# Two layers of a hybrid diffusion trunk on one core: when the neighbourhood biases are asked for

## The chip, the cores and the metric

One core of a Trainium2 chip runs the whole program: TensorE (PE, with its weight loads as PEld), VectorE (DVE), ScalarE (ACT), GpSimd (POOL), SyncE (SP) and 16 DMA engines that all queues share. The metric is device time in microseconds (us) of one execution; lower is better. Of the runs shown the median counts.

## The reference, cut to what matters

Two layers over 256 latent tokens and, in the first layer alone, 256 context tokens, width 1024. Each layer multiplies the modulated, normalised tokens by one input projection and splits the result into three groups of heads: windowed attention (4 heads, here two pairs, A(0) and A(1)), a state space scan (8 heads, gated by `z`), and neighbourhood attention (4 heads, two pairs, N(0) and N(1)). For a neighbourhood head

```
sc = einsum(q, k) * scale + bias[rpb]     # 256 x 256, -1e30 outside the window
p  = softmax(concat([sc, s_ctx]))         # s_ctx: scores against 256 context tokens
o  = p_loc @ v + p_ctx @ v_ctx
```

The bias depends on weights alone, so its 256 x 256 table per head is laid out ahead of time and lies in device memory as `in_nab_dram`. The three groups are concatenated and multiplied by an output projection; then follow a router and a mixture of 32 gated experts (per token two of the eight experts of one group). The six shift, scale and gate rows of each layer (`mods` in the code) are the product of the conditioning with an 1024 x 6144 matrix, streamed from memory in slabs of 1 MB.

## The kernel before, in words

`mixers(l)` (l is 0 for the first layer, 1 for the second) does a layer's heads, `projection_and_experts(l)` what follows. Everything is unrolled; a planner (the framework's scheduler) simulates the program with costs of its own, and writes a fixed order for each engine: an instruction that is earlier in the program has priority among those whose inputs are ready in that simulation. On the chip each engine, and each queue of transfers, keeps that order and waits at whatever is not there yet.

One pair of heads is `attn_pair` (L797 to L845). For each of two blocks of 128 queries: scores of both heads by TensorE into two PSUM banks `sc`, for N pairs the bias added by VectorE (L815, one 128 x 512 instruction per block), the maximum (L817), `exp` by ScalarE into `pr` (L827), the division (L835), four transposes by TensorE into PSUM bank `tp` (L838), and a copy of these into a buffer `PT` (L839, by a helper that lets ScalarE, L238, and VectorE, L240, take turns). After both blocks 16 matmuls multiply `PT` with the values (L843, into `tp` again), and a copy takes the result to `oT`. `tp` is one bank, and the transposes of the output gate (`natural(9, z_post)`, L753) and of the state space norm (`ssd_gate`, L778 and L783) use it as well.

`PT` buffers have the tag `t4`, of which there are four (L273). A pair takes two. The biases `nb` (one tile of 128 x 2 x 2 x 256 for a pair, 0.5 MB) take one each, and so do the masks `M` of the state space scan, four for each of its chunks, which are done before attention begins. A tile gets its buffer in the order in which the program asks for tiles of that tag, and waits until one is free.

`attn_N(i)` (L860) asks for its bias at its own start: a tile `nb`, and two transfers of 256 KB on ScalarE's queue (L863). In the second layer the order of the program is A(0), three steps of `mods`, A(1), three steps of `mods`, N(0), three steps, `natural(9, z_post)`, `ssd_gate(0)`, N(1), and the rest of `mods`. A step of `mods` is eight matmuls (L116, L119) on one slab `m`; there is one buffer for `m`, so the next slab is loaded (L1662, on SP's queue) only when these are done. SP's queue also carries the weights: of the output projection (L88) and of the experts (L1004).

The output projection of the second layer starts inside this stretch: its first products (L1197) need A's and N(0)'s outputs, the following ones (L1206 to L1208) the gated state space output.

Of the kernel before, what the change touches and what calls it, by code (L numbers as in the profile page):

```python
# [44 lines left out]
def backbone(ctx: ExitStack, tc, I, out, dbg=None):  # L45
    nc = tc.nc
# [213 lines left out]
    def mixers(l):  # L260
# [3 lines left out]
        with ExitStack() as es:  # L264
# [7 lines left out]
            def t4(shape, name, dtype=F32):  # L272
                return tp.tile([P] + shape, dtype, tag="t4", name=name, bufs=4)  # L273
# [466 lines left out]
            def z_tile(i, p):  # L740
                silu_half(oT(2 + i), p, NTK)

            def natural(u, post):

                ws = [wunit(l, u), wunit(l, u + 1)]
                outs = [ps("mm"), ps("mm")]
                wN(ws, 512, outs)
                for t, p in enumerate(outs):
                    y = s2([512], "yn")
                    dst = post(y, p)  # L750
                    tr = ps("tp", (P, 4, P))
                    for c in range(4):
                        T.transpose(tr[:, c, :], y[:, c * P:(c + 1) * P], ident)  # L753
                    for j, d_ in enumerate(dst):
                        n = 4 // len(dst)
                        pcopy(d_[:, :, t * P:(t + 1) * P], tr[:, j * n:(j + 1) * n, :])
# [9 lines left out]
            def ssd_gate(s):  # L766
                seg = slice(s * 256, (s + 1) * 256)
                pn = ps("tp")
                y2s = []
                for g in range(2):  # L770
                    zs = oT(2 + 2 * g, seg, 2)
                    V.tensor_tensor(zs, zs, xc[:, 2 * g:2 * g + 2, seg], op=ALU.mult)
                    y2 = s2([2, 256], "y2")
                    S.activation(y2, zs, AF.Square)
                    y2s.append(y2)
                for i in range(2):
                    for ct in range(4):
                        T.matmul(pn[:, i:i + 1], y2s[ct // 2][:, ct % 2, i * P:(i + 1) * P], ones[:, 0:1],  # L778
                                 start=(ct == 0), stop=(ct == 3))
                rn = rstd_of(sm, pn[:, 0:2], 512, 2)  # L780
                pb = ps("tp")
                for i in range(2):
                    T.matmul(pb[:, i * P:(i + 1) * P], rn[:, i:i + 1].to_broadcast([P, P]), ident,  # L783
                             start=True, stop=True)
                for ct in range(4):
                    V.scalar_tensor_tensor(oT(2 + ct, seg), oT(2 + ct, seg), gcol[:, ct:ct + 1], pb[:, 0:256],
                                           op0=ALU.mult, op1=ALU.mult)


            def rope(x_):  # L790
                sh = s2([256], "sh")
                V.stream_shuffle(sh, x_, [i ^ 16 for i in range(32)])
                V.tensor_tensor(sh, sh, M_("sin"), op=ALU.mult)
                V.tensor_tensor(x_, x_, M_("cos"), op=ALU.mult)
                V.tensor_tensor(x_, x_, sh, op=ALU.add)
# [59 lines left out]
            def attn_A(i):  # L855
                attn_pair(kA, 0, (0, 64), i, sinks=snk[:, i:i + 3:2], wmask=True)
                if need_ctx:
                    attn_pair(kA, 1, (0, 64), i, sinks=snk[:, i:i + 3:2])

            def attn_N(i):  # L860
                nb = t4([2, 2, 256], "nb")
                for hf in range(2):
                    nc.scalar.dma_start(nb[:, hf], I["nab"][l, 2 * i + hf])  # L863
                vo = (128 + 128 * i, 128 + 128 * i + 64)
                attn_pair(kN[:, i], 0, vo, 6 + i, bias=nb)
                if need_ctx:
                    attn_pair(kN[:, i], 1, vo, 6 + i)

            def q_tile(i, p):
                S.activation(oT(i), p, AF.Copy, scale=0.125)  # L870

            if need_ctx:
                tl = Tiles([(5, 0), (5, 1), (6, 0), (6, 1), (7, 0), (7, 1), (8, 0), (8, 1), (9, 0), (9, 1), (10, 0)])

                def tile_():
                    p = tl.next()
                    mods(l, 1)
                    return p

                S.copy(kA, tile_())  # L880
                rope(kA[:, 0:256])
                q_tile(0, tile_())
                rope(oT(0, slice(0, 256)))
                q_tile(1, tile_())
                rope(oT(1, slice(0, 256)))
                S.copy(kN[:, 0], tile_())
                attn_A(0)
                attn_A(1)
                q_tile(6, tile_())
                q_tile(7, tile_())  # L890
                S.copy(kN[:, 1], tile_())
                attn_N(0)
                for i in range(4):
                    z_tile(i, tile_())
                ssd_gate(0)
                ssd_gate(1)
                attn_N(1)
            else:
                tl = Tiles([(5, 0), (5, 1), (6, 0)])
                S.copy(kA, tl.next())  # L900
                rope(kA[:, 0:256])
                S.copy(kN[:, 0], tl.next())
                S.copy(kN[:, 1], tl.next())
                mods(l, 2)
                natural(7, q_post)
                mods(l, 2)
                rope(oT(0, slice(0, 256)))
                rope(oT(1, slice(0, 256)))
                attn_A(0)
                mods(l, 3)  # L910
                attn_A(1)
                mods(l, 3)
                attn_N(0)
                mods(l, 3)
                natural(9, z_post)
                ssd_gate(0)
                attn_N(1)
# [752 lines left out]
    def mods(l, n):  # L1670
        for _ in range(n):
            next(rest[l], None)

    for l in range(2):
        oT = mixers(l)
        projection_and_experts(l, oT)
# [163 lines left out]
```

## Time and profile before

| what | value |
|---|---|
| median of 3 runs | 1119.57 us (1114.42 to 1122.86) |
| the profiled execution | 1124.72 us, of which span 1122.8 us |
| mean granted TensorE clock | 0.953 of full |
| PE busy | 1005.9 us, 90% of the span |
| DVE, ACT, POOL busy | 589.0, 280.5, 187.3 us |
| moved by DMA | 321.69 MB, mean 286 GB/s |

The profiled execution is 5.15 us longer than the median, so a sum made in its trace is a difference, to be taken from either. The granted clock is in tenths or hundredths of full speed: 1.00 is 2.4 GHz, 0.50 is 1.2 GHz. In the bracket behind a row stands how long its engine was idle just before it and what ended that.

### The profile page before, as it was taken

The page shows a single profiled execution, that of the slowest core. Times are in us where ns is not written, and L with a number is a line of the kernel's source. Part 1 is how long each engine was busy: PE and PEld are TensorE (multiplying, and loading weights), DVE is VectorE, ACT ScalarE, POOL GpSimd, SP SyncE. Part 2 cuts the span into 40 slices and gives each one's busy share as a digit, 9 for nine tenths or more (in the row PEclk, how much of TensorE's full clock was granted, in tenths as well). Part 3 has the DMA queues.
Part 4 walks back from the last instruction along what each step waited for, and adds up shares of the span by engine and source line. Part 5 has one row for each costly group of instructions (what it writes and reads, how often), then busy time and mean ns, then how long its engine had stood idle before and what let it go on. Part 6 is the DMA issues. An engine that isn't in the chain of part 4 may idle for free. (4 is left out here: it accounts for less than half of the span.)

```text
span 1122.8 us, 13571 instructions
## 1 busy us (share of the span) xinstructions
PE 1005.9 (90%) x5041; PEld 533.5 (48%) x5041; DVE 589.0 (52%) x1208; ACT 280.5 (25%) x567; POOL 187.3 (17%) x181
## 2 busy tenths in 40 slices
PE   6996899999998699988898798999789799999995
PEld 4684455456565233322343586564355444444342
DVE  5679695763557334322366687766434522322353
ACT  3242111442421112111122552133321211111112
POOL 2106270000214211111121404300010100000011
PEclk9997999999999799999999899899888899999998
DMA  9756545438195899999998534346748689999992
GB/s 378 287 214 244 225 151 185 154 136 330 65 382 207 295 405 424 424 425 425 426 415 313 182 113 150 130 149 220 306 153 360 239 344 424 424 425 424 424 400 81
DMA packets 60009, 321.69 MB, mean 286 GB/s; under 512 B 11899, under 2 KB 12795, under 8 KB 26584
## 3 DMA queue, kind: packets, MB, share of 16 engines
q1 hardware_dynamic: 51152, 305.57, 68.7%
q0 software_dynamic: 6048, 11.08, 2.7%
q10 hardware_dynamic: 2728, 4.02, 1.0%
q8 instruction: 44, 0.72, 0.3%
q14 instruction: 37, 0.30, 0.1%
HBM read 316.84 MB, written 22.09 MB: 302 GB/s over the span
## 5 line engine op out<-in xcount | busy, mean ns | idle before, releaser
L389 PE MATMUL mm<-x,sp 128*128 128x512 f32 (+1 forms) x176 | 73.5, 418 | 0.1
L391 PE MATMUL mm<-x,sp 128*128 128x512 f32 (+1 forms) x176 | 72.3, 413 | 0.3 <-DVE sp L249 0.3
L390 PE MATMUL mm<-x,sp 128*128 128x512 f32 (+1 forms) x176 | 71.5, 407 | 0.6 <-DVE alg L547 0.4
L1407 PE MATMUL mm<-w,xT 128*64 128x512 f32 x208 | 62.7, 596 | 6.1 <-DMA w<-in_wexp_dram 6.1
L1407 PE MATMUL mm<-w,xg__7943 128*64 128x512 f32 x216 | 66.0, 596 | 0.0
L1474 POOL DMA_INDIRECT yd<-y,irow x24 | 23.8, 991 | 215.6 <-DVE y L1473 206.6
L1414 DVE SCALAR_TENSOR_TENSOR hg<-hg,mm 128x256 f32<-128x256 f32 x32 | 13.4, 418 | 77.3 <-ACT hg L1413 77.3
L248 ACT CAST sp<-w 128x1024 fp32r<-128x1024 f32 (+1 forms) x42 | 42.5, 1013 | 34.7 <-PE mm L391 11.5
L249 DVE TENSOR_TENSOR sp<-w,sp 128x1024 fp32r<-128x1024 f32 (+1 forms) x36 | 44.8, 1246 | 9.6 <-ACT sp L248 9.5
L1413 ACT ACTIVATE hg<-mm 128x256 f32<-128x256 f32 x32 | 12.3, 384 | 147.9 <-PE mm L1407 147.9
L116 PE MATMUL mod<-m,cc 128*32 128x512 f32 x80 | 42.7, 616 | 5.3 <-DMA m<-in_wmod_dram 3.2
L240 DVE COPY xT<-sp 128x512 f32<-128x512 f32 x16 | 11.0, 690 | 67.3 <-PE sp L1399 67.3
L1407 PE MATMUL mm<-x,xg__7943 128*64 128x512 f32 x128 | 44.7, 597 | 0.0
L119 PE MATMUL mod<-m,cc 128*32 128x512 f32 x240 | 43.2, 616 | 0.0
L218 POOL TENSOR_TENSOR rs<-ms,nhalf 128x1 f32<-128x1 f32 (+2 forms) x13 | 9.3, 713 | 196.4 <-DVE mx L822 111.0
L389 PEld LDWEIGHTS mm<-x,sp 128*128 128x128 f32 x176 | 34.1, 194 | 15.4 <-issue 8.0
L827 ACT ACTIVATE pr<-sc,mx 128x512 f32<-128x512 f32 (+1 forms) x48 | 29.3, 616 | 46.8 <-DVE mx L822 43.8
L391 PEld LDWEIGHTS mm<-x,sp 128*128 128x128 f32 x176 | 34.1, 194 | 11.9 <-issue 5.6
L566 DVE SCALAR_TENSOR_TENSOR yh<-xp,cw,yh 128x512 f32<-128x512 f32 (+1 forms) x48 | 35.0, 728 | 8.8 <-ACT yh L564 7.2
L390 PEld LDWEIGHTS mm<-x,sp 128*128 128x128 f32 x176 | 34.2, 195 | 9.6 <-issue 4.0
L1322 POOL DMA_INDIRECT xg__2845<-h2d,itok x16 | 16.9, 1055 | 112.5 <-PE sp L1399 101.3
L1407 PEld LDWEIGHTS mm<-w,xg__7943 128*64 128x64 f32 x216 | 19.3, 137 | 31.5 <-issue 30.2
(1054 smaller groups left out, 2443.4 us busy)
## 6 DMA issues: line engine op xcount, KB each, us to landing
w<-in_wexp_dram SPq DMA_DIRECT2D x74, 1024.0 KB
x<-in_wexp_dram SPq DMA_DIRECT2D x46, 1024.0 KB
m<-in_wmod_dram SPq DMA_DIRECT2D x42, 1024.0 KB
w<-in_win_dram SPq DMA_DIRECT2D x21, 1024.0 KB
sp<-in_wexp_dram SPq DMA_DIRECT2D x20, 1024.0 KB
tb<-in_wexp_dram SPq DMA_DIRECT2D x11, 1024.0 KB
m<-in_wexp_dram SPq DMA_DIRECT2D x10, 1024.0 KB
xn<-in_wexp_dram SPq DMA_DIRECT2D x8, 1024.0 KB
```

Of the source, the lines that this page charges most:

```text
L116: line(first())
L119: line(other())
L248: S.copy(wh, w)
L249: eng.tensor_tensor(wl, w, wh.bitcast(F32), op=ALU.subtract)
L389: T.matmul(p[:, :n], wh[:, k], xh(k, slice(0, n))[:, 0], start=(k == 0), stop=False)
L390: T.matmul(p[:, :n], wh[:, k], xl(k, slice(0, n))[:, 0], start=False, stop=False)
L391: T.matmul(p[:, :n], wl[:, k], xh(k, slice(0, n))[:, 0], start=False, stop=(k == KD - 1))
L566: V.scalar_tensor_tensor(yh[:, :ns], xp[:, :ns, k:k + 256], cw[:, ct, k:k + 1], yh[:, :ns], op0=ALU.mult, op1=ALU.add)
L827: S.activation(pr[:, :n], sc[:, hf, :n], AF.Exp, bias=mx[:, hf:hf + 1], accum_out=l_[:, hf:hf + 1])
L1322: fetch_line(G.indirect_dma_start(xg_[:, p_ % 2, :], None, h2d[0:nt * P, :], bass.IndirectOffsetOnAxis(ap=itok[:, p_:p_ + 1], axis=0), bou ...
L1407: behind(T.matmul(ph[64 * e:64 * e + 64, :], xT[:, k, 64 * e:64 * e + 64], ws[e][k // 4][k % 4 // 2][:, k % 2 * 512:k % 2 * 512 + 512], st ...
L1474: fetch_line(G.indirect_dma_start(yd[l][0:2 * nt * P, :], bass.IndirectOffsetOnAxis(ap=irow[:, p_:p_ + 1], axis=0), y, None, bounds_check= ...
```

## The change

A function `bias_N` asks for the biases of the pairs that it is given, and `attn_N` takes the tile from a table. In the second layer both are asked for behind A(0) and ahead of A(1), so that they lie in two of the four `t4` buffers while A(1) and N(0) run; in the first layer that of N(0) is asked for between A(0) and A(1), and that of N(1) right behind N(0). What is computed is the same.

```diff
+            nbs = {}
+
+            def bias_N(*which):
+
+                for i in which:
+                    nbs[i] = t4([2, 2, 256], "nb")
+                    for hf in range(2):
+                        nc.scalar.dma_start(nbs[i][:, hf], I["nab"][l, 2 * i + hf])
+
             def attn_N(i):
-                nb = t4([2, 2, 256], "nb")
-                for hf in range(2):
-                    nc.scalar.dma_start(nb[:, hf], I["nab"][l, 2 * i + hf])
+                nb = nbs[i]
...
                 attn_A(0)
+                bias_N(0)
                 attn_A(1)
                 q_tile(6, tile_())
                 q_tile(7, tile_())
                 S.copy(kN[:, 1], tile_())
                 attn_N(0)
+                bias_N(1)
...
                 attn_A(0)
                 mods(l, 3)
+                bias_N(0, 1)
                 attn_A(1)
```

## Rows read from the trace of the kernel before

**Rows 1.** Tile view of the bias, whole execution: cause, us idle, times.

```profile
DMA nb<-in_nab_dram: 10.6, 2
```

**Rows 2.** Chain of waits, second layer: start us, us, what.

```profile
795.90 10.27 DMA nb<-in_nab_dram
```

**Rows 3.** Timeline of DVE, second layer: start us, us, instruction, [idle before].

```profile
770.50 0.68 DVE L240 COPY PT<-tp 128x512 f32<-128x512 f32 x1
...
780.42 0.68 DVE L240 COPY PT<-tp 128x512 f32<-128x512 f32 x1
...
786.91 1.30 DVE L815 TENSOR_TENSOR sc<-sc,nb 128x512 f32<-128x512 f32 x2 [1.66 <-DMA nb<-in_nab_dram]
...
789.25 0.41 DVE L240 COPY oA<-tp 128x256 f32<-128x256 f32 x1
...
806.25 1.30 DVE L815 TENSOR_TENSOR sc<-sc,nb 128x512 f32<-128x512 f32 x2 [8.94 <-DMA nb<-in_nab_dram]
```

**Rows 4.** Timeline of PE (matmuls), second layer, same columns.

```profile
776.27 1.95 PE L843 MATMUL tp<-PT,vt 128*64 128x256 f32 x16
778.58 0.62 PE L116 MATMUL mod<-m,cc 128*32 128x512 f32 x1
792.20 0.62 PE L116 MATMUL mod<-m,cc 128*32 128x512 f32 x1 [0.78 <-DMA m<-in_wmod_dram]
...
799.25 0.66 PE L838 MATMUL tp<-cst,pr 128*128 128x128 f32 x4
799.74 1.88 PE L1197 MATMUL mm<-w,oA 128*128 128x512 f32 x4
808.19 3.68 PE L843 MATMUL tp<-PT,vt 128*64 128x256 f32 x16 [6.57 <-DVE PT L240]
811.80 2.74 PE L1197 MATMUL mm<-w,oA 128*128 128x512 f32 x4
...
816.63 0.62 PE L116 MATMUL mod<-m,cc 128*32 128x512 f32 x1
...
820.35 3.58 PE L778 MATMUL tp<-masks,y 128*128 128x1 f32 x16 [2.06 <-ACT y L774]
```

**Rows 5.** Stretches: PE, PEld, DVE, ACT, POOL busy us, clock, DMA share, GB/s.

```profile
220.00:230.00 10.00, 10.00 (x62) 6.04 (x62) 7.57 (x24) 6.07 (x17) 0.00 (x0) 1.00 0.47 179
785.00:790.00 5.00, 5.00 (x34) 2.96 (x27) 3.34 (x7) 0.56 (x2) 0.00 (x0) 1.00 1.05 431
800.00:806.00 6.00, 1.62 (x4) 0.38 (x2) 0.00 (x0) 0.00 (x0) 0.00 (x0) 1.00 1.02 423
806.00:813.00 7.00, 4.81 (x18) 2.40 (x19) 4.35 (x7) 1.86 (x6) 0.00 (x0) 0.54 0.37 157
820.00:830.00 10.00, 7.52 (x30) 5.04 (x31) 2.04 (x6) 1.69 (x4) 2.13 (x3) 0.51 0.44 185
920.00:1060.00 140.00, 137.76 (x674) 56.89 (x670) 38.30 (x72) 18.70 (x41) 9.66 (x10) 1.00 1.01 424
```

**Rows 6.** Timeline of ACT and its queue: bias requests and what stands near.

```profile
233.07 0.84 ACTq L863 DMA_DIRECT2D nb<-in_nab_dram  x2
773.03 0.20 ACT L831 ACTIVATE es__7287<-es__7287 128x2 f32<-128x2 f32 x1 [4.64 <-DVE es__7287 L821]
781.97 0.59 ACT L238 COPY PT<-tp 128x512 f32<-128x512 f32 x1 [2.52 <-PE tp L838]
782.05 0.85 ACTq L863 DMA_DIRECT2D nb<-in_nab_dram  x2
795.51 0.88 ACTq L863 DMA_DIRECT2D nb<-in_nab_dram  x2
```

**Rows 7.** Timeline of SP's queue, second layer.

```profile
773.54 6.49 SPq L1662 DMA_DIRECT2D m<-in_wmod_dram  x2
...
785.76 0.33 SPq L1662 DMA_DIRECT2D m<-in_wmod_dram  x1
...
799.38 0.33 SPq L1662 DMA_DIRECT2D m<-in_wmod_dram  x1
```

## The prediction

> **What bounds the kernel now.** I began with the only thing that the change moves, the bias, in the tile view over the whole execution: its additions waited for the transfers 10.6 us, twice in all [rows 1]. Both times are in the second layer [rows 3]: 1.66 us ahead of N(0)'s additions, 8.94 us ahead of N(1)'s. The first layer's four additions never waited, so nothing is to be gained there.
>
> Then the chain of waits, to see whether either wait set the end. N(1)'s is on it, as the second transfer's whole flight of 10.27 us [rows 2]; N(0)'s is not. Next the engines' orders at that place. VectorE stands at N(1)'s additions until 806.25, and behind them in its order is the copy of N(0)'s last transposes. TensorE made those at 799.25 and needs the copy for N(0)'s products with the values, so it stands from 801.62 (799.74 + 1.88) to 808.19, 6.57 us [rows 4]. From 802 on no engine computes [rows 5]: a bias for work that comes last holds up work that comes first.
>
> The windows add the clock. TensorE was still granted 1.00 after it had stood for over 4 us, and 0.54 on the mean over the following stretch [rows 5]. The two groups of matmuls behind the stall took 3.68 and 2.74 us [rows 4]; the same shapes took 1.95 (A(0)'s products, 776.27) and 1.88 at full clock.
>
> Last I asked whether later stages give time back. In the expert stage the DMA engines are full, 424 GB/s, but TensorE is busy 137.76 of 140 us [rows 5], and the loads there are issued as its work frees buffers. A shift at 808 us should therefore reach the end.
>
> **Where the requests go.** Each old request stands on ScalarE's queue just behind a copy into the second `PT` buffer of the pair before it (782.05 behind 781.97, [rows 6]): it had to wait its turn for a `t4` buffer. By the same rule the new requests stand behind the first copy into A(0)'s second buffer, at 770.50 [rows 3]: four transfers, 1.05 MB, issued by about 772.5. They are needed at 786.91 and 797.31 (806.25 less 8.94), so 14 and 25 us later; the slowest transfer seen took 10.27.
>
> **The change part by part**, in the profiled execution (1124.72 us, 5.15 above the median).
>
> 1. N(1)'s wait. Without it VectorE adds from 797.31 to 798.6 and is free when the transposes end at 799.91; the copy (0.68) is done by 800.7, before TensorE's present work ends at 801.62. All 6.57 us go. What is late next is the following `mods` group, at 816.63 [rows 4], now some 9 us earlier: its slab is asked for at 799.38 [rows 7], and slabs took 6.44 us at most (785.76 to 792.20). That gives 805.8 against 807.4: close, but no wait.
> 2. The clock. With TensorE at full speed there the two groups give back 3.68 - 1.95 and 2.74 - 1.88, 2.59 us. A second slow stretch follows, 0.51 from 820 to 830, after a gap of 2.06 us [rows 4, 5]. That gap belongs to the gate's chain and stays, so I take 0 there; the bound is 3.7 us, half of the 7.52 us busy.
> 3. N(0)'s wait of 1.66. Behind it TensorE is busy 5.00 of 5 us [rows 5], which covers it; without that cover it is worth its 1.66. But TensorE then waits 0.78 us for a slab at 792.20 [rows 4], loaded while 431 GB/s flowed, and the 0.52 MB of bias leave that stretch (1.2 us at that rate). I take 0.8, between 0 and 1.7.
> 4. The same bytes earlier. They now run beside the slab asked for at 773.54 [rows 7] and used at 778.58 [rows 4]. 1.05 MB at 424 GB/s delay it by at most 2.5 us; the requests leave 1 to 3 us ahead of it, so I take 0.5 lost.
> 5. ScalarE issues four transfers, 0.85 us for two [rows 6], so 1.7 us. It was idle 4.64 us before 773.03 [rows 6]: nothing. Without that cover its `exp` for A(0)'s second block would be 1.7 us late.
> 6. Buffers. While both biases lie, pairs share the other two: A(1)'s first copy must wait until A(0)'s products have read `PT`. That is a new wait, with later copies of either engine behind it. But the products end at 778.22 and that copy starts at 780.42 [rows 3, 4], since transposes and products take turns in one `tp` bank in any case. Nothing, with 2.2 us of slack for this and the following pairs.
> 7. The planner's order. N(0)'s scores no longer wait, in its simulation either, so it may put N(0)'s softmax further ahead. At A(1)'s pace (first copy 780.42, output copied at 789.25, so 8.8 us) a pair that begins its copies right there, 789.25, has its output at 798.1; fixed order gives 801.62 + 1.95 = 803.6. That is 5.5 us at most, and 0 at least if TensorE, full in that stretch, only swaps work; below 0 too, for an order written for one set of arrival times may suit another less: -2. Nearest is the full TensorE: I take 1.0.
> 8. First layer. N(0)'s request moves up from 233.07 [rows 6] into ScalarE's `exp`s, 0.84 us. TensorE is busy 10.00 of 10 there [rows 5], which hides it, at worst it costs 0.84; N(1)'s stays behind N(0)'s copies.
>
> Sum: 6.57 + 2.59 + 0.8 - 0.5 + 1.0 = 10.5 us. From the profiled execution 1114.2; from the median 1109.1.
>
> **A rule against it.** Asking for the same bytes at another time buys nothing when DMA engines are what is short: step 4, at worst 2.5 us lost. The Trainium skill (DMA: Bandwidth & Descriptors, "Issuing engines are not separate DMA queues") says just that: transfers started by ScalarE and by SyncE run on the same 16 engines and interleave. The trace agrees: 0.52 MB of bias took 10.27 us while 423 GB/s flowed. By the rule alone a transfer put beside a slab slows the slab, and the sum would be 8.5.
>
> **Rivals.**
> - *N(0) and the gate move up together.* With N(0)'s output at 798.1 and TensorE never slowed, step 7 takes its upper end, and the gate starts that much sooner. For it: VectorE's wait at 786.91 shows that N(0)'s scores were there before its bias. Against it: one `m` buffer paces the `mods` groups among which this work stands. Gain 10.5 - 1.0 + 5.5 = 15, to 1104.6; with step 2's bound up to 18.7.
> - *The stall only changes its name.* The `mods` group of 816.63 is planned at 801.6, and TensorE waits for its slab until 805.8 to 808.6, where the queue ran empty (0.37 of 7 us from 806 on [rows 5]). It stands 4.2 to 7.0 us in place of 6.57; up to 2.4 us and up to the 2.59 of the clock are left: gain 0 to 5, middle 3, so 1116.5. Against it: in the present order N(0)'s products and eight products L1197 stand ahead of that group (808.19 to 816.63).
> - *The request does not move*, because no two `t4` buffers are free or the planner writes it late anyway: 0, 1119.6. For it: the old requests stood late for want of a turn. Against it: the masks were read before attention began, and A(0) holds two of four.
> - *Slower: `mods` in a row.* If, with its gaps filled, the planner puts the last three groups close together, each waits a full slab flight, 6.44 us, since the next slab is asked for only when the last is used; and each such wait slows what follows as the present one does, 2.59. Three of these, 27 us, less 10.5: 16.6 slower, 1136. It decides from less than 6.4 us of other work between two groups; now the slab asked for at 799.38 is used 17 us later, at 816.63.
>
> **Numbers.** About 1%, 11.2 us, is what a measurement can tell. The forecast, 1109, has 0.46, of which 0.19 lies beyond 1%; the first rival 0.28; the renamed stall 0.15; no move 0.06; the slower one 0.05 (0.04 beyond 1%). Faster 0.47, same 0.49, slower 0.04. The forecast's own range: down to a gain of 5.5 with steps 4 and 7 at their worst (10.5 - 2.0 - 3.0), up to 13.7 with step 3 at its best and half of step 7's upper end (0.9 and 2.3 more), so 1106 to 1114. The whole range takes in the first rival with 3 us to spare and the renamed stall, runs of one kernel lying 4 us either way: 1102 to 1117.
>
> **What would show it.** The bias additions without a wait for DMA; requests near 771; TensorE without a gap between the first products L1197 and N(0)'s products, and those 1.95 us long; 1.00 where 0.54 stood. TensorE waiting over 3 us for `m` behind 800 would prove the second rival, a wait for `m` at each of three groups the slower one. The prediction is wrong if the gap is gone and the expert stage still starts at the same time.

## The result, and the profile after

Before: 1120.48 us, median of 4 runs (1114.42 to 1122.86). After: 1105.92, median of 4 (1103.66 to 1107.64). The ratio is 0.9865, with a 95% interval of 0.983 to 0.990: 14.6 us faster, where 10.5 were forecast. Timed again later, the changed kernel took 1102.69 us against 1119.28, ratio 0.9854 (0.983 to 0.988). The profiled execution of after took 1105.33 us, its span 1103.5; the two profiled executions are 19.4 us apart, and the first question is how much of this belongs to the change. In one kernel further down, that with only N(0)'s bias early, one execution of 3811.74 us is left out of the median.

Lines behind the edit are higher in the changed kernel: by 4 at the request (L863 is L867), by 10 from the output projection on (L1197 is L1207, L1044 is L1054, L1185 is L1195, L1227 is L1237). The tile view of the bias, where [rows 1] had 10.6 us:

```profile
L867 ACTq DMA_DIRECT2D nb<-in_nab_dram x8: 334/404/1111, 215.1 to 770.1; - x8
L815 DVE TENSOR_TENSOR sc<-sc,nb x8: 686/692/700, 236.1 to 797.9; 128x512 f32<-128x512 f32 x8
its engine sat idle before it (us, times) until:
  PE sc L119: 0.8, 2
```

No addition waits for a transfer any more. In the timeline of VectorE (start us, us, instruction) N(0)'s two additions stand ahead of the split L249, where in [rows 3] they stood at 786.91; N(1)'s have moved from 806.25:

```profile
776.62 0.69 DVE L815 TENSOR_TENSOR sc<-sc,nb 128x512 f32<-128x512 f32 x1
...
779.97 0.70 DVE L815 TENSOR_TENSOR sc<-sc,nb 128x512 f32<-128x512 f32 x1 [0.30 <-PE sc L119]
...
783.43 1.22 DVE L249 TENSOR_TENSOR sp<-w,sp 128x1024 fp32r<-128x1024 f32 x1
...
795.53 0.69 DVE L815 TENSOR_TENSOR sc<-sc,nb 128x512 f32<-128x512 f32 x1
```

TensorE's timeline of after answers to [rows 4]:

```profile
777.21 0.62 PE L116 MATMUL mod<-m,cc 128*32 128x512 f32 x1 [1.33 <-DMA m<-in_wmod_dram]
797.12 1.95 PE L843 MATMUL tp<-PT,vt 128*64 128x256 f32 x16
799.00 1.98 PE L1207 MATMUL mm<-w,oA 128*128 128x512 f32 x4
803.43 0.60 PE L753 MATMUL tp<-cst,yn 128*128 128x128 f32 x4
803.86 1.88 PE L1207 MATMUL mm<-w,oA 128*128 128x512 f32 x4
805.68 0.62 PE L116 MATMUL mod<-m,cc 128*32 128x512 f32 x1
806.67 1.95 PE L778 MATMUL tp<-masks,y 128*128 128x1 f32 x16
830.43 0.66 PE L1237 MATMUL sp<-cst,x 128*128 128x128 f32 x4 [1.38 <-DVE x L1198]
830.92 3.60 PE L1195 MATMUL mm<-w,oA 128*128 128x512 f32 x8
834.36 1.02 PE L1195 MATMUL mm<-sp,oA 128*128 128x512 f32 x2
835.32 1.94 PE L1054 MATMUL tp<-wr,mc 128*128 128x36 f32 x16
```

N(0)'s products come without a wait and take 1.95 us, the stall of 6.57 and its 3.68 are gone. But two things changed that no bias waits for. The gate's L778, which waited 2.06 us for y and took 3.58, now has four L1207 and a `mods` group between it and the last transposes L753, waits for nothing and takes 1.95. And the router's matmuls with `wr` stand behind ten L1195. In the timeline of before, not shown so far, they stood ahead:

```profile
845.93 0.33 PE L1227 MATMUL sp<-cst,x 128*128 128x128 f32 x1 [1.72 <-DVE x L1188]
847.17 3.35 PE L1044 MATMUL tp<-wr,mc 128*128 128x36 f32 x16 [0.92 <-DMA wr<-in_wr_dram]
850.33 0.88 PE L1227 MATMUL sp<-cst,x 128*128 128x128 f32 x3
851.00 5.25 PE L1185 MATMUL mm<-w,oA 128*128 128x512 f32 x8
```

TensorE stood 0.92 us for `wr`, and the sixteen and the eight matmuls that follow took 3.35 and 5.25 us in place of 1.94 and 3.60. (The trace shows each instruction of L1044, L1185 and L1197 as two matmuls; the expectations and the orders below count instructions.)

To sum this up, one window from A(0)'s first scores of the second layer to the first matmul of the experts (stretch, its length, busy time of PE, PEld, DVE, ACT and POOL, granted clock, DMA share, GB/s). Before, then after:

```profile
760.70:891.50 130.80, 108.05 (x534) 60.33 (x535) 67.11 (x207) 38.03 (x86) 9.16 (x13) 0.87 0.66 251
```

```profile
758.17:871.60 113.43, 100.12 (x533) 55.99 (x534) 66.18 (x207) 37.94 (x86) 9.02 (x13) 0.92 0.75 290
```

The stretch is 17.37 us shorter: TensorE stands 22.75 - 13.31 = 9.44 us less, and the same matmuls take 7.93 us less, since more of them run at the higher of the clock's two levels, 2.4 GHz and not 1.2. Behind it the pair gives nothing back: 231.3 us to the span's end before, 231.9 after. Ahead of it after is 2.53 us earlier; that is run to run, since the traced kernels with the first layer of before reach A(0) between 754.40 and 760.70, those with the first layer of after between 754.67 and 758.17.

One slow stretch stays. The gate's chain still has two waits of 1.05 and 1.09 us in after, and behind them the granted clock falls again (timeline of TensorE, then a stretch in the columns above):

```profile
809.66 0.71 PE L783 MATMUL tp<-cst,rs 128*128 128x128 f32 x4 [1.05 <-POOL rs L218]
811.47 0.79 PE L1216 MATMUL mm<-x 128*128 128x512 f32 x1 [1.09 <-ACT x L1212]
```

```profile
813.17:818.17 5.00, 5.00 (x20) 3.61 (x23) 1.71 (x3) 1.78 (x4) 0.00 (x0) 0.59 0.01 3
```

### The profile page after: what moved, and what is told of

It is laid out like the page before. It is cut to its first block, busy times and chain, and to the rows that moved or that the text cites. A ratio compares the mean times of both kernels' runs of the same rounds, so it can differ in the third digit from the quotient of the medians.

```text
span 1103.5 us, 13572 instructions
## 1 busy us (share of the span) xinstructions
PE 999.2 (91%) x5041; PEld 528.2 (48%) x5041; DVE 589.3 (53%) x1208; ACT 280.3 (25%) x567; POOL 188.0 (17%) x181
## 5 line engine op out<-in xcount | busy, mean ns | idle before, releaser
L249 DVE TENSOR_TENSOR sp<-w,sp 128x1024 fp32r<-128x1024 f32 (+1 forms) x36 | 44.8, 1246 | 10.4 <-ACT sp L248 10.3
L116 PE MATMUL mod<-m,cc 128*32 128x512 f32 x80 | 42.7, 616 | 4.7 <-DMA m<-in_wmod_dram 4.7
```

The source lines that it names most:

```text
L116: line(first())
L249: eng.tensor_tensor(wl, w, wh.bitcast(F32), op=ALU.subtract)
```

## The experiments

Each row was timed beside runs of before, in five batches, so rows of different batches are to be compared by their ratios rather than by their medians. "Stretch" is the window from A(0)'s first scores to the experts, in one trace of each kernel, "idle" its length less TensorE's busy time.

| kernel | us, median | ratio to before, 95% interval | stretch | busy | idle |
|---|---|---|---|---|---|
| before | 1119 to 1121 | | 130.80 | 108.05 | 22.75 |
| first layer alone | 1118.86 | 0.9979 (0.9960 to 0.9997) | 130.86 | 108.55 | 22.31 |
| router later | 1116.63 | 0.9960 (0.9935 to 0.9985) | 127.49 | 103.71 | 23.78 |
| order kept | 1112.06 | 0.9921 (0.9888 to 0.9955) | 122.40 | 105.39 | 17.01 |
| order kept, router later | 1109.66 | 0.9891 (0.9854 to 0.9927) | 119.61 | 103.48 | 16.13 |
| the same, gate filled | 1105.85 | 0.9881 (0.9854 to 0.9908) | 117.49 | 101.93 | 15.56 |
| only N(0)'s bias early | 1107.55 | 0.9868 (0.9837 to 0.9899) | 119.29 | 105.40 | 13.89 |
| only N(1)'s bias early | 1105.66 | 0.9872 (0.9845 to 0.9900) | 114.84 | 101.14 | 13.70 |
| after | 1105.92 | 0.9865 (0.9830 to 0.9901) | 113.43 | 100.12 | 13.31 |
| after, again | 1102.69 | 0.9854 (0.9826 to 0.9882) | 113.43 | 100.11 | 13.32 |
| second layer alone | 1102.30 | 0.9843 (0.9814 to 0.9871) | 113.70 | 100.83 | 12.87 |
| ahead of A(0) | 1106.46 | 0.9872 (0.9835 to 0.9909) | 116.80 | 103.36 | 13.44 |
| ahead of A(0), router later | 1101.41 | 0.9840 (0.9811 to 0.9868) | 112.83 | 101.21 | 11.62 |

**The two layers apart.** Second layer alone, and first layer alone:

```diff
                 attn_A(0)
-                bias_N(0)
                 attn_A(1)
...
                 attn_N(0)
-                bias_N(1)
```

```diff
                 mods(l, 3)
-                bias_N(0, 1)
                 attn_A(1)
```

A bias not asked for by then is asked for at its pair's own start.

> The second layer's half of the change alone: both biases in front of A(1) there, the first layer's requests where the kernel before has them. Theory (the whole gain is the second layer's): the time of the changed kernel, 1106, 14.5 us under the kernel before. Rival (the first layer gives something too, since in the changed kernel's trace A(0)'s first scores of the second layer stood 2.5 us earlier than before, ahead of every request moved there): 1108.5, and A(0)'s first scores back near 760.7.

> The first layer's half alone: N(0)'s request in front of A(1), N(1)'s in front of the z tiles; the second layer as before. Theory (the whole gain is the second layer's): 1120.5, no difference. Rival (the first layer gives something too): 1118, 2.5 us under the kernel before.

The second layer alone has the whole gain, 17.9 us under before's median; the 2.5 us that A(0) stood earlier are not the first layer's, since here, with the first layer of before, A(0) stood at 754.40. The first layer alone comes out 1.4 us lower, an effect at the edge of what can be told. Its stretch is that of before to 0.06 us, but that stretch lies behind the edit, so it doesn't settle this.

**One bias early.** In the second layer:

```diff
-                bias_N(0, 1)
+                bias_N(1)      # the other kernel: bias_N(0)
```

> As the changed kernel, but in the second layer only N(1)'s bias is asked for in front of A(1); N(0)'s request stands at N(0)'s own start. Theory (about two thirds of the gain is N(1)'s wait with the clock behind it, the rest comes from N(0)'s softmax and the gate moved ahead, which needs N(0)'s bias early): 9 us under before, 1111.5; N(0)'s additions behind the split and with a wait of up to 1.7 us. Rival (N(1)'s wait and clock carry all): 1106, as the changed kernel.

> As the changed kernel, but in the second layer only N(0)'s bias is asked for in front of A(1); N(1)'s request stands at N(1)'s own start. Theory (N(0)'s early softmax and the gate are worth about 5 us by themselves): 1115, with N(1)'s additions still waiting, since 10 us of flight lie behind a request that stands near N(0)'s copies. Rival (N(0)'s bias is worth only its covered wait, 0.8 at most): 1119.7, the stall of TensorE near 6 us still there.

By the times, either bias alone brings the whole gain, within the intervals. In the first kernel the rival had the time, in the second both missed it by 7 us or more: N(0)'s early softmax is not worth 5 us on top of the rest. In the kernel with only N(1)'s bias early N(0)'s additions waited longer than in before (timeline of VectorE):

```profile
784.93 1.30 DVE L815 TENSOR_TENSOR sc<-sc,nb 128x512 f32<-128x512 f32 x2 [3.84 <-DMA nb<-in_nab_dram]
```

and N(0)'s products began at 800.77, 43.7 us behind A(0)'s scores against 39.0 in after; yet the stretch is only 1.4 us longer than in after. With N(0)'s alone, N(1)'s additions still waited:

```profile
795.53 0.70 DVE L815 TENSOR_TENSOR sc<-sc,nb 128x512 f32<-128x512 f32 x1 [2.80 <-DMA nb<-in_nab_dram]
```

but N(0)'s last copy, at 791.35, was ahead of that wait on VectorE. In before, VectorE's wait for N(1)'s bias stood ahead of N(0)'s last copy; in neither of these kernels does it. That this is what matters fits both, but was not tested by itself. In the trace of the kernel with N(0)'s bias alone the stretch is 5.9 us longer than in after, so that it has the whole gain rests on the times, whose intervals are 7 to 8 us wide.

**Waits without reordering.** The second layer's requests early, with the instructions of TensorE, VectorE, ScalarE and SyncE in exactly the order of before (each entry of `ORDER` holds the instructions of TensorE, VectorE or ScalarE in that order, and SyncE's queue has it in the trace too; the dependence sets order and no wait):

```diff
+                bias_N(0, 1)
                 attn_A(1)
...
+            for one in ORDER if l else ():
+                names = [f"I-{i_}" for i_ in one.split()]
+                for i_, ahead in zip(names[1:], names):
+                    tc.add_manual_dep(nc.get_inst_by_name(i_), ahead,
...
```

> The second layer's half of the change, with the instructions of TensorE, VectorE, ScalarE and of SyncE's queue held in exactly the order of the kernel before; only the four bias requests stand earlier on ScalarE's queue. What is left of the gain is the waits and the clock, without any reordering. In the traces so far, from A(0)'s scores of the second layer to the experts, idle time of TensorE fell by 9.4 us and its busy time, for the same matmuls, by 7.9. Theory A (the planner's order is worth what lies beyond the stall of 6.6 us and the slow clock just behind it; the waits for y ahead of L778, 2.1 us, and for wr ahead of L1044, 0.9 us, stay, and with each of them a slow stretch): 9.5 us under before, 1110.5. Theory B (both later waits and their slow stretches are the stall's own after-effects and go with it): 1104, as the planner's own order. Rival (order is all, the bias waits only reappear as others): 1117 or more.

Theory A. The gain is 8.65 us by the medians and 8.4 in the stretch. The timeline of TensorE in this kernel (L123 is before's L116, L785 its L778, L1059 its L1044, L1200 its L1185):

```profile
775.51 0.62 PE L123 MATMUL mod<-m,cc 128*32 128x512 f32 x1 [1.82 <-DMA m<-in_wmod_dram]
798.02 1.95 PE L850 MATMUL tp<-PT,vt 128*64 128x256 f32 x16
799.90 1.98 PE L1212 MATMUL mm<-w,oA 128*128 128x512 f32 x4
807.68 2.95 PE L785 MATMUL tp<-masks,y 128*128 128x1 f32 x16 [2.06 <-ACT y L781]
834.44 2.21 PE L1059 MATMUL tp<-wr,mc 128*128 128x36 f32 x16 [0.76 <-DMA wr<-in_wr_dram]
837.13 4.75 PE L1200 MATMUL mm<-w,oA 128*128 128x512 f32 x8
```

The stall is gone with its slow clock; the waits for y and `wr` stay, to within 0.2 us. They are not after-effects of the stall. Of the matmuls behind them, L785 (2.95 us for 3.58 in before) and the first eight L1200 (4.75 for 5.25) stay slow, while L1059 is nearly as fast as in after (2.21 for 3.35). How slow these are changes from trace to trace: in the kernel with only the router's group moved, whose order is that of before up to there, the same wait was followed by a faster group:

```profile
818.55 2.10 PE L785 MATMUL tp<-masks,y 128*128 128x1 f32 x16 [2.06 <-ACT y L781]
```

**The router's group.** In that order, and in before's with the late biases, one group of TensorE moved:

```diff
-  L1044 x8, L1227 x3, L1185 x5, L1185 x3
+  L1227 x3, L1185 x5, L1044 x8, L1185 x3
```

> The kernel before, biases late as they were, every engine's order as before but for one group: the eight matmuls of L1044 (which wait for wr) stand on TensorE behind four L1227 and five L1185 instead of ahead of them, as in the changed kernel. Theory (that wait and the slow stretch behind it are worth something by themselves: 0.9 us idle, 1.4 us in L1044, 1.65 us in the first eight L1185): 3.5 to 4 us under before, 1116.5. Rival (the clock falls there anyway, since TensorE stands 1.7 us for x just ahead): 0 to 1 us, 1120.

> Both edits together: the order of before kept, the second layer's biases early, and the one group of L1044 moved behind the five L1185. Theory A: the two gains add, 13 to 13.5 us under before, 1107; what is then left to the changed kernel's 1106 is the gap ahead of the gate. Theory B (everything hangs on the stall): 1104, no different from order kept alone.

With the biases late, the move alone gives 4.1 us, as expected. Timeline of TensorE in that kernel (L1192 is before's L1185, L1051 its L1044):

```profile
842.87 0.66 PE L1234 MATMUL sp<-cst,x 128*128 128x128 f32 x4 [1.72 <-DVE x L1195]
843.36 3.60 PE L1192 MATMUL mm<-w,oA 128*128 128x512 f32 x8
847.66 1.87 PE L1051 MATMUL tp<-wr,mc 128*128 128x36 f32 x16
```

The wait of 1.72 us for x is the same as before and the matmuls behind it are fast; so that wait alone did not cost the clock. Whether the second wait, for `wr`, did or the narrow matmuls of L1044 that stood just behind it, the move doesn't part, since it takes both away. On the kept order the move is worth 2.4 us by the medians, 2.8 in the stretch. Both edits together give 11.1 us by the medians, under the 13 expected and the 12.7 of the two apart, but within the intervals: the gains add as far as can be told.

**The gate's gap.** On top of that, TensorE's order between N(0)'s products and the gate made that of the changed kernel:

```diff
-  L1197 x2, N(0)'s products, L1197 x2, L753 x4, L1197 x2, mods, L753 x4, L778
+  N(0)'s products, L1197 x2, L753 x4, L1197 x2, L753 x4, L1197 x2, mods, L778
```

> As order kept with L1044's group moved (biases early, order of before), and one more group moved on TensorE: the second four transposes L753 stand ahead of the last four L1197 and the mods group instead of behind them, and N(0)'s products ahead of one pair of L1197, as in the changed kernel; so 2.9 us of other matmuls lie between those transposes and the gate's L778, which waited 2.1 us for y. Theory A (that gap and the slow stretch behind it are the last third of the gain): the wait for y is gone, L778 takes 1.95 us instead of 3.1, and the time falls by 3 to 4 us, from 1109.7 to 1106, 14 us under before. Rival (the gate's remaining gaps of 1.0 and 1.1 us slow the clock in any case): 1 us at most, 1108.5.

The median, 1105.85, is the one expected, but the ratio moved only from 0.9891 to 0.9881 and the two intervals cover each other; the stretch is 2.1 us shorter. The wait for y was halved, not removed (0.97 of 2.06), and N(0)'s products now waited 0.78 us for VectorE's copy. When the gate's matmuls begin, only 0.5 of these 2.1 us is there (51.37 us behind A(0)'s scores, 51.83 without the move), since the new wait takes back most of the 1.1 us that the shorter one gives. Another 1.0 is L785, 2.10 us in place of 3.12, and that may be the trace's own, since it took 2.10 us behind the full wait too (above). So the shorter wait is shown in the trace; that the reordering gains 2 us is not, and the times alone don't show it.

**Earlier still.** The second layer alone, with both biases one pair earlier:

```diff
+                bias_N(0, 1)
                 attn_A(0)
                 mods(l, 3)
-                bias_N(0, 1)
                 attn_A(1)
```

> As the second layer alone, but both biases are asked for ahead of A(0), one pair earlier, with an order of the planner's own. Theory (the requests in front of A(1) delay one slab, for which TensorE waits 1.3 to 1.6 us there): that wait is gone and the time is 1 to 1.5 us lower, 1101. Rival (the same 1.05 MB then delays an earlier slab or a weight load by as much): 1102, with a wait for m or w of 1 us or more before A(0).

Neither. The slab's wait is gone (TensorE waits 0.2 us for `m` in all), but `wr`, which SyncE asks for at 820.25, behind a row of 1 MB loads, is now late by 3.61 us, since the planner's order here has the router's group ahead of the other ten again:

```profile
825.99 3.62 PE L1052 MATMUL tp<-wr,mc 128*128 128x36 f32 x16 [3.61 <-DMA wr<-in_wr_dram]
829.42 1.09 PE L1235 MATMUL sp<-cst,x 128*128 128x128 f32 x4
830.31 5.79 PE L1193 MATMUL mm<-w,oA 128*128 128x512 f32 x8
```

The same kernel with its order held, and the router's eight matmuls behind the next ten:

> As the biases asked for ahead of A(0), every engine's order held as it was there, but for TensorE's eight matmuls of L1052, which waited 3.6 us for wr: they stand behind four L1235 and six L1193. Theory (that kernel lost to the wait for wr, with the slow stretch behind it, what it had gained from the slab's wait): the wait falls from 3.6 us to under 1, the first eight L1193 from 5.79 to 3.6, so 4.5 to 5 us under that kernel's 1106.5: 1102, below the changed kernel. Rival (the gate's stretch or the router's takes the clock down in any case): 1105.

> The changed kernel once more, on the same chip and beside the same runs of before as the kernel with the router's matmuls moved. 1106, 14.5 us under before.

The eight L1193 took 3.60 us again (L1200 there) and the wait for `wr` is gone. The median fell by 5 us to 1101.41, the ratio from 0.9872 to 0.9840, with intervals that overlap; the stretch is 4.0 us shorter. The slab's wait, which this kernel's requests should have removed, was 0.99 us again, where the kernel before it had none. 1101.41 is the lowest median, but its interval covers that of the changed kernel measured beside it, 1102.69: no version is shown to beat it.

## Why the prediction was right in its time and wrong in one step

The gain forecast, 10.5 us, lies 4.1 below the one measured; the time that came out is nearly that of the first rival, 1104.6. It stands at the lower edge of the forecast's own range, 1106 to 1114, and inside the whole one, which had been widened for that rival: that the time fits is in part luck, since one term was taken at about a sixth of what it turned out to be. By steps:

1. **N(1)'s wait**: right. With the order kept, all 6.57 us go, and the `mods` group behind has its slab (805.68 in after, no wait).
2. **The clock**: right for the stall. With the order kept, 3.68 and 2.74 became 1.95 and 1.98, 2.49 us for 2.59. Of the second slow stretch, taken at 0 since "that gap belongs to the gate's chain and stays", the gap does stay in that order (2.06 us, L785 2.95 us). In the planner's new order the gap of 2.06 is gone and L778 takes 1.95 us, but the clock falls all the same some 3 us later, behind the chain's other waits (0.59 from 813.17 to 818.17).
3. **N(0)'s wait**: small, as taken. The slab's wait of 0.78 at 792.20 became 0.41 in after (783.50) and 0.51 with the order kept.
4. **Contention**: perhaps under-sized. 0.5 was taken; TensorE's wait for that slab was 1.33 us in after and 1.82 with the order kept, inside the bound of 2.5. In after the slab was asked for at 770.67 and used at 777.21. The rule weighed there (the Trainium skill, DMA: Bandwidth & Descriptors, "Issuing engines are not separate DMA queues") says that transfers of ScalarE and SyncE share the 16 engines, and a slower slab beside the biases would agree with it. But these runs don't show that the biases are the cause: in the kernel with only the router's group moved the biases were asked for late, at 779.97 and 793.50, and TensorE waited about as long for the same slab, asked for at 769.77:

```profile
776.50 0.62 PE L123 MATMUL mod<-m,cc 128*32 128x512 f32 x1 [1.63 <-DMA m<-in_wmod_dram]
```

Without step 7 the forecast's sum is 9.5 us, the rule's 7.5; the kept order gave 8.65, between them, which decides for neither.
5. and 6. **ScalarE and the buffers**: nothing, as taken. The requests stand at 767.78 and 769.71, behind the copy of 767.62, and no copy of A(1) waits for `PT`.
7. **The planner's order**: this step failed. It was taken at 1.0 us, with 5.5 as its upper end, for N(0)'s softmax moved ahead. Holding the order shows what it is worth: 1112.06 less 1105.92, 6.1 us by the medians (ratios 0.9921 against 0.9865 and, timed again, 0.9854), and 122.40 less 113.43, 9.0 in the profiles. And the way was another. N(0)'s early softmax is not needed, since the kernel without it has the same time within the intervals. The order gained where work was put into two holes tens of us behind the requests: the router's group (2.8 us of the stretch, 2.4 to 4.1 us in times) and the gate's (at most 2.1 of the stretch). The last 4.1 us of the stretch, between the kernel with both moves and after, were not taken apart by an experiment. In the traces 2.2 of them lie ahead of N(0)'s products, which begin 41.16 us behind A(0)'s first scores with both moves and 38.95 in after; so what step 7 had in mind, N(0)'s work further ahead, may be worth up to that.
8. **First layer**: 0 taken, 1.4 us better measured, at the edge of what can be told.

With steps 2, 3 and 4 at their sizes in the kept order, 6.57 + 2.49 + 0.27 - 1.82 = 7.5 us, against 8.65 by the medians and 8.4 in the stretch; the rest is not taken apart, and the clock behind the later waits can move the stretch by as much. The error was to read the waits for y and for `wr` as properties of the kernel, when they were properties of one order that the planner would write anew.

The *first rival* had the time right and half of its mechanism: the gate did move up (the end of L778 from 823.93 to 808.62), but N(0)'s early output is not needed for the gain: where N(0)'s products came at 43.7, later than with the order kept (41.9), the time was the same as after's within the intervals. The *renamed stall* did not come: TensorE waits 0 us for `m` between 800 and 817 in after. That *the request does not move* is refuted by its place, *`mods` in a row* by the waits for `m` of 1.9 us in all, three times, where 6.4 each were feared.

Open: why the planner left those two holes while the biases were late, and filled or shortened them once either was early. Its forecast times were not looked at; only its orders were.

## What to carry to other kernels

Where a planner writes the order, split a removed wait into two terms and measure them apart: the wait itself with every engine's order held, and what the new order does elsewhere; here the second was about 6 of 14.6 us. Read TensorE's waits over the whole stretch behind the edit, not only those of the thing edited: here the router's hole of 0.9 us gave 2.4 to 4.1 us when other work was put ahead of it, the gate's of 2.1 us at most that. Before a wait is put down to an edit, look for it in a trace without that edit: the slab's wait was there too. And asking still earlier was no gain by itself, since the planner wrote yet another order, with the router's group ahead once more and TensorE waiting for `wr`.

## What the runs showed of the hardware that was not expected

In before, a wait of 0.92 us for `wr`, with 0.33 us of work between it and one of 1.72 for x, was followed by more loss in clock than in standing: 1.41 us in the sixteen matmuls and 1.65 in the eight behind them. The 1.72 us alone, in the kernel with only that group moved, and 1.38 us in after, cost nothing in the eight wide matmuls behind them.

The clock behind a wait is not the same each time: behind the same 2.06 us for y, in the same order of TensorE around it, the gate's sixteen matmuls took 3.58, 3.12, 2.95 and 2.10 us in four traces. A gain of 1 us read there from one trace is not yet one.

A bias transfer of 0.26 MB, the second of N(1)'s pair, landed 10.27 us after its request in before, where it left beside 1 MB loads; in the second-layer kernel, where the requests stand ahead of A(1), transfers landed 5.0 to 5.3 us after theirs. A slab of 1 MB was late by 1.63 us with the bias requests late, and TensorE's wait for it was 0 to 1.8 us over the traces, so a single wait of this size is no measure of contention.
